# Encoder layer in split fp32: the order of copies, splits and statistics in the first feed-forward chunk

## The chip, the cores and the metric

The kernel runs on one core of one Trainium2 chip. The metric is the device time of one execution in microseconds (us), the median of three runs. Lower is better. Engines are named as in the profile: PE multiplies matrices, ACT is the scalar engine, DVE the vector engine, POOL the GpSimd engine, SP the queue that issues nearly all loads.

## The reference

One encoder layer over 256 tokens of width 2048, all in fp32. The part that the change touches is the beginning of the first line:

```python
h = h + 0.5 * swiglu(rmsnorm(h, ffn1_norm), ffn1_w_gate, ffn1_w_up, ffn1_w_down)   # D_FF = 5632
u = rmsnorm(h, mix_norm); z = u @ w_in           # neighbourhood attention, MLA, two gates
h = h + (sigmoid(gate_A) * A + sigmoid(gate_B) * Bm) @ w_out
h = h + 0.5 * swiglu(rmsnorm(h, ffn2_norm), ffn2_w_gate, ffn2_w_up, ffn2_w_down)
h = h + sigmoid(rmsnorm(h, pl_norm) @ w_pl_gate) * (p @ w_pl)
out = rmsnorm(h, final_norm)

def swiglu(x, w_gate, w_up, w_down):
    return (silu(x @ w_gate) * (x @ w_up)) @ w_down
```

## The kernel before

**Split products.** PE takes operands rounded to fp32r. Every fp32 operand is therefore split in two: `hi` is the rounded copy, made by ACT, and `lo` is what is left, subtracted by DVE (`split`, lines 87 to 89). A product is three matmuls, lo by hi, hi by hi and hi by lo (`triple`, lines 92 to 95). So each weight that comes from memory costs PE three matmuls, ACT one cast and DVE one subtraction.

**Granules.** The work is a list `grans` of granules, g0, g1 and so on, each a few tiles of weights with their matmuls. A loop over the list (the end of the function) emits for granule g its matmuls, then the small tasks that are noted for step g (`tasks[g]`, in the order in which they were noted; `at(d, fn)` notes one for d steps later), and calls `convert()`, which loads and splits weights of later granules as far as buffers W0 to W5 are free: about three granules ahead. Each engine executes its own instructions in the order in which they were emitted. The order of emission is therefore the order of every queue.

**The first chunk.** The feed-forward has 11 chunks of 512 columns. Chunk 0 is done in the plain way: g0 to g7 multiply the 16 K-tiles of the gate weights (two K-tiles a granule, 12 matmuls of 512 columns), g8 to g15 those of the up weights. The gate sums stand in PSUM banks 0 and 1, the up sums in banks 2 and 3. From g16 on, chunks 1 to 3 use a scheme with fewer products (`Block`): eight pieces of four weight tiles a chunk, five of them `Plain` (24 matmuls), three of them split over `SevenA` (9 matmuls) and `SevenB` (12). Its sums stand in banks 0 to 6. The first `Plain` granule, g16, adds first into banks 4, 5 and 6 (18 matmuls), and then into bank 3 (6 matmuls), which has to be free of the up sums by then.

**Inputs of the products.** x is transposed by PE (`plain_tiles`, four transposes into one PSUM bank), scaled by the norm's gain, and split. `first_forms(i)` does this for pair i of the eight pairs of K-tiles: tile `X{i}` gets the four plain pieces, hi and lo. The block scheme needs linear combinations too, `more_forms(i)`: DVE adds and subtracts the plain pieces into `e` (`sums`), and `e` is split into the rest of `X{i}`; the sums of pairs 2, 4 and 6 are four pieces, of the others two. The sums are taken from an fp32 copy of the plain pieces, `zs` (in buffers Z and H3), which `keep` writes from PSUM. g0 to g7 need the plain pieces of pair 0 to 7, in this order, g8 to g15 again, and g16 on need the combinations.

**Before the change.** `first_forms(i)` has ACT write hi from PSUM (line 382, two instructions), DVE write lo from PSUM (line 384, two instructions), and ACT write the fp32 copy from PSUM (line 390, two instructions). Pairs 0 and 1 are done before the loop, pairs 2 to 7 at steps 0 to 5. The statistics of the norm (`late_stat`, squares on ACT, line 413, two for each quarter of the row) stand at steps 3 to 6, the reciprocal root (`stat_done`, 14 small DVE instructions) at the end of step 6. `gate_evac` (sigmoid on ACT, one product on DVE, for each of two halves) follows the last gate matmul of g7 at once. `more_forms(0)` to `more_forms(7)` stand at steps 8 to 15, sums and split together. `gains(16, 72)`, which transposes the other norms' gains, stands at step 7. `up_evac` (line 540, two DVE instructions) follows the last up matmul of g15; two steps on, `tr(0)` and `tr(1)` transpose its result.

Of the kernel before, what the change touches and what calls it, by code (L numbers as in the profile page):

```python
# [7 lines left out]
F32 = mybir.dt.float32  # L8
F32R = mybir.dt.float32r
I32 = mybir.dt.int32  # L10
AF = mybir.ActivationFunctionType
# [3 lines left out]
P = 128  # L15
# [12 lines left out]
def encoder_kernel(ctx, tc, x, p, ffn1_norm, ffn1_w_gate, ffn1_w_up, ffn1_w_down, mix_norm, w_in,  # L28
# [8 lines left out]
    tmp = ctx.enter_context(tc.tile_pool(name="tmp", bufs=2))  # L37
    psum = ctx.enter_context(tc.tile_pool(name="psum", bufs=1, space=bass.MemoryType.PSUM))

    V, S, G, PE = nc.vector, nc.scalar, nc.gpsimd, nc.tensor  # L40
    count = [0]

    def nm(s):
        count[0] += 1
        return f"{s}_{count[0]}"
# [6 lines left out]
    def piece(tag, shape, dt=F32):  # L52
        return mem.tile(shape, dt, tag=tag, name=nm(tag))
# [10 lines left out]
    def bank():  # L64
        if seven_on[0]:
            return psum_tile(7)
        turn["side"] += 1
        return psum_tile(4 + turn["side"] % 4)
# [11 lines left out]
    tasks = {}  # L80
# [3 lines left out]
    def at(d, fn):  # L84
        tasks.setdefault(step[0] + d, []).append(fn)

    def split(hi, lo, r):
        S.copy(hi, r)  # L88
        V.tensor_tensor(out=lo, in0=r, in1=hi.bitcast(F32), op=ALU.subtract)  # L89
# [83 lines left out]
    def unit(*a, **k):  # L173
        Unit(*a, **k)
# [110 lines left out]
    for nme, g in (("ffn1", ffn1_norm), ("mix", mix_norm), ("ffn2", ffn2_norm), ("pl", pl_norm),  # L285
                   ("qa", q_a_norm), ("kva", kv_a_norm)):
        n = g.shape[-1] // P
# [7 lines left out]
    gT = cst.tile([P, 72], F32, name="gT")  # L295

    def gains(a, b):
        gps = bank()
        PE.transpose(gps[:, 0:b], grow[0:b, :], ident[0:b, 0:b])
        V.tensor_copy(gT[:, a:b], gps[:, a:b])  # L300
# [34 lines left out]
    forms = {}  # L335
# [36 lines left out]
    zs = {}  # L372

    def first_forms(i):
        p2 = plain_tiles(i)
        if i % 4 == 0:
            zs[i // 4] = piece(("Z", "H3")[i // 4], [P, 4, 4, P])
        f = piece(f"X{i}", [P, 2, 8 if i in SEVEN else 6, P], F32R)
        forms[i] = f
        hi, lo = [[f[:, b, 2 * k:2 * k + 2, :].rearrange("p a b -> p (a b)") for k in range(2)] for b in range(2)]  # L380
        for k in range(2):
            S.activation(hi[k], p2[:, k], AF.Copy, scale=gT[:, 2 * i + k:2 * i + k + 1])
        for k in range(2):
            V.scalar_tensor_tensor(out=lo[k], in0=p2[:, k], scalar=gT[:, 2 * i + k:2 * i + k + 1],
                                   in1=hi[k].bitcast(F32), op0=ALU.mult, op1=ALU.subtract)

        def keep():
            z = zs[i // 4][:, i % 4].rearrange("p (k a) b -> p k (a b)", k=2)
            for k in range(2):
                S.activation(z[:, k], p2[:, k], AF.Copy, scale=gT[:, 2 * i + k:2 * i + k + 1])  # L390
        return keep

    def more_forms(i):
        e = tmp.tile([P, 4, P], F32, tag="s", name=nm("e"))
        m = sums(zs[i // 4][:, i % 4], e, i)
        split(forms[i][:, 0, 4:4 + m], forms[i][:, 1, 4:4 + m], e[:, 0:m, :])

    def first_xop(kt):
        f = forms[kt // 2]
# [72 lines left out]
    def ffn(phase, wg, wu, wd, nxt):  # L472
        hT = {}

        def block(c):
            a = {}

            def early(q):
                a["u"], a["v"] = tmps("t")
                a["w"], a["c"] = tmps("pt")  # L480
                S.copy(a["u"], q[1])
                V.tensor_tensor(out=a["w"], in0=q[6], in1=a["u"], op=ALU.add)
                V.tensor_tensor(out=a["v"], in0=q[7], in1=a["w"], op=ALU.add)

            def late(q):
                r = rstd[phase]
                s = tmps("s")

                def first():
                    V.tensor_tensor(out=a["u"], in0=q[2], in1=a["u"], op=ALU.add)  # L490
                    V.tensor_tensor(out=a["c"], in0=q[4], in1=a["v"], op=ALU.add)

                def rest():
                    S.activation(s[0], a["u"], AF.Sigmoid, scale=r[:, 0:1])
                    S.activation(s[1], a["c"], AF.Sigmoid, scale=r[:, 1:2])
                    V.tensor_tensor(out=a["v"], in0=q[5], in1=a["v"], op=ALU.subtract)
                    V.tensor_tensor(out=a["w"], in0=q[5], in1=a["w"], op=ALU.subtract)
                    V.tensor_tensor(out=a["w"], in0=q[3], in1=a["w"], op=ALU.add)
                    for t, (g, o) in enumerate((("u", "w"), ("c", "v"))):
                        V.scalar_tensor_tensor(out=s[t], in0=a[g], scalar=r[:, t:t + 1], in1=s[t],  # L500
                                               op0=ALU.mult, op1=ALU.mult)
                        V.scalar_tensor_tensor(out=a[o], in0=a[o], scalar=r[:, t:t + 1], in1=s[t],
                                               op0=ALU.mult, op1=ALU.mult)

                    def tr(j):
                        def f():
                            if j == 0:
                                hT[c] = piece(f"H{c % 4}", [P, 2, 4, T], F32R)
                            transpose_chunk([a["w"], a["v"]], hT[c], js=(j,))
                        return f  # L510
                    at(2, tr(0))
                    at(3, tr(1))
                return first, rest
            b = Block([rows(wg, c * 512), rows(wu, c * 512)], form, early, late)

        def down_evac(n, final):
            def f(ps):
                for t in range(2):
                    hs = h[:, t, n * 512:n * 512 + 512]
                    V.scalar_tensor_tensor(out=hs, in0=ps[t], scalar=0.5, in1=hs, op0=ALU.mult, op1=ALU.add)  # L520
                if final:
                    next_norm(nxt, n)
            return f

        hold = {}

        def gate_evac(ps):
            r = rstd[phase]
            hold["a"] = tmps("t")
            for t in range(2):  # L530
                s = tmp.tile([P, 512], F32, tag="s", name=nm("s"))
                S.activation(s, ps[t], AF.Sigmoid, scale=r[:, t:t + 1])
                V.scalar_tensor_tensor(out=hold["a"][t], in0=ps[t], scalar=r[:, t:t + 1], in1=s,
                                       op0=ALU.mult, op1=ALU.mult)

        def up_evac(ps):
            r = rstd[phase]
            a = hold.pop("a")
            for t in range(2):
                V.scalar_tensor_tensor(out=a[t], in0=ps[t], scalar=r[:, t:t + 1], in1=a[t],  # L540
                                       op0=ALU.mult, op1=ALU.mult)

            def tr(j):
                def f():
                    if j == 0:
                        hT[0] = piece("H0", [P, 2, 4, T], F32R)
                    transpose_chunk(a, hT[0], js=(j,))
                return f
            at(1, tr(0))
            at(2, tr(1))  # L550

        for c0, c1 in PARTS:
            for c in range(c0, c1):
                if grans:
                    block(c)
                else:
                    unit(rows(wg, 0), 16, 512, first_xop, gate_evac)
                    unit(rows(wu, 0), 16, 512, first_xop, up_evac)
            down = len(grans)
            for n in range(4):  # L560
                def hop(kt, c0=c0):
                    d = hT[c0 + kt // 4]
                    return d[:, 0, kt % 4, :], d[:, 1, kt % 4, :]
                unit(rows(wd[c0 * 512:c1 * 512], n * 512), 4 * (c1 - c0), 512, hop,
                     down_evac(n, c1 == NC_FF), wide=True, align=(n == 0))
            m = c1 - c0
            g = grans[down:down + 2 * m]
            grans[down:down + 2 * m] = g[:m - 1] + g[m:2 * m - 1] + [g[m - 1], g[2 * m - 1]]
# [525 lines left out]
    keep = [first_forms(0)]  # L1094
    for _ in range(14):
        PE.transpose(idle[:, 0:P], ident, ident)
    for a, b in ((256, 512), (512, 1024), (1024, 1536)):
        convert()
        nc.sync.dma_start(h[:, :, a:b], xr[:, :, a:b])
        if a == 256:  # L1100
            keep.pop()()
            first_forms(1)()

    def late_stat(n):
        def f():
            stat_chunk("ffn1", n)
            if n == 3:
                stat_done("ffn1")
        return f
    for i in range(2, 8):  # L1110
        tasks.setdefault(i - 2, []).append(lambda i=i: first_forms(i)())
    for n in range(4):
        tasks.setdefault(3 + n, []).append(late_stat(n))
    for i in range(8):
        tasks.setdefault(8 + i, []).append(lambda i=i: more_forms(i))
    tasks.setdefault(7, []).append(lambda: gains(16, 72))

    for g, e in enumerate(grans):
        step[0] = g
# [58 lines left out]
```

## Time and profile before

| what | value |
|---|---|
| median of three runs | 2202.64 us (2202.17 to 2203.82) |
| profiled execution, device time | 2200.09 us |
| profiled execution, span of the trace | 2198.2 us |
| mean granted PE clock | 0.996 |
| PE busy | 2168.6 us (99%) |
| DVE busy | 1550.7 us (71%) |
| ACT busy | 1068.0 us (49%) |
| read from memory | 409.83 MB |

The span counts from the first to the last instruction that the profiler recorded. A line of the timeline has start, length, engine, line of the kernel, operation, output and inputs, count, and in square brackets the time for which the engine stood idle before it and what ended the idle time. A line of the waits has who waited, for whom, microseconds in total, times, and the longest. A line of the windows has the stretch, its length, and the busy time of PE, of its weight loads (PEld), of DVE, ACT and POOL, each with a count of instructions, then the granted PE clock, the busy share of the DMA engines and GB/s.

### The profile page before, as it was taken

How to read it: one execution, taken by the hardware profiler on the slowest of the kernel's cores; microseconds unless marked ns; L12 is line 12 of the kernel's file. 1: busy time of each engine (PE TensorE's matmuls, PEld its weight loads, DVE VectorE, ACT ScalarE, POOL GpSimd, SP SyncE). 2: the span in 40 equal slices, each digit the busy share in tenths (PEclk: the TensorE clock that was granted, in tenths of full speed). 3: DMA queues.
4: the chain of work that ended last, by engine and by line, in shares of the span. 5: the costliest groups of instructions: out<-in, count | busy, mean ns of one | idle time of the engine just before them, and what ended most of it. 6: DMA issues, size and time to landing. Idle time of an engine off the chain costs nothing. (4 is left out here: it accounts for less than half of the span.)

```text
span 2198.2 us, 24815 instructions
## 1 busy us (share of the span) xinstructions
PE 2168.6 (99%) x9789; PEld 1787.7 (81%) x9789; DVE 1550.7 (71%) x1601; ACT 1068.0 (49%) x1100; POOL 35.8 (2%) x39
## 2 busy tenths in 40 slices
PE   8899999999999999999999999999999999999997
PEld 6688888888888887788888888788888888888886
DVE  5798579975897565545655556899659994698565
ACT  6555344543555454444544445555435553455453
POOL 0000000000000000050000000000000000000000
PEclk9999999999999999999999999999999999999999
DMA  6565555565565554375455555555655666566453
GB/s 213 168 215 202 197 186 182 192 229 192 173 205 204 175 172 154 115 212 189 147 179 191 191 173 200 183 191 192 221 181 184 208 203 210 172 212 232 163 192 125
DMA packets 212003, 413.53 MB, mean 188 GB/s; under 512 B 11656, under 2 KB 12240, under 8 KB 211760
## 3 DMA queue, kind: packets, MB, share of 16 engines
q1 hardware_dynamic: 210640, 408.46, 55.8%
q0 software_dynamic: 1216, 3.50, 0.7%
q8 instruction: 76, 1.25, 0.2%
q14 instruction: 39, 0.32, 0.0%
q10 hardware_dynamic: 32, 0.01, 0.0%
HBM read 409.83 MB, written 2.10 MB: 187 GB/s over the span
## 5 line engine op out<-in xcount | busy, mean ns | idle before, releaser
L89 DVE TENSOR_TENSOR W<-R,W 128x1024 fp32r<-128x1024 f32 (+2 forms) x633 | 1008.1, 1604 | 460.6 <-ACT W L88 459.1
L88 ACT CAST W<-R 128x1024 fp32r<-128x1024 f32 (+2 forms) x633 | 855.7, 1358 | 858.7 <-DVE R L240 275.0
L93 PE MATMUL B<-W,X 128*128 128x512 f32 x2113 | 834.1, 395 | 11.3 <-DVE t L540 6.9
L95 PE MATMUL B<-W,X 128*128 128x512 f32 x2113 | 824.6, 390 | 4.4 <-DVE W L89 4.4
L94 PE MATMUL B<-W,X 128*128 128x512 f32 x2113 | 823.4, 390 | 0.0
L93 PEld LDWEIGHTS B<-W,X 128*128 128x128 f32 x2113 | 397.2, 188 | 95.9 <-DVE t L540 7.3
L95 PEld LDWEIGHTS B<-W,X 128*128 128x128 f32 x2113 | 397.0, 188 | 90.7 <-DVE W L89 7.2
L94 PEld LDWEIGHTS B<-W,X 128*128 128x128 f32 x2113 | 397.4, 188 | 80.1
L93 PE MATMUL B<-W,H 128*128 128x512 f32 x832 | 325.7, 392 | 0.0
L95 PE MATMUL B<-W,H 128*128 128x512 f32 x832 | 324.1, 389 | 0.0
L94 PE MATMUL B<-W,H 128*128 128x512 f32 x832 | 323.8, 389 | 0.0
L95 PEld LDWEIGHTS B<-W,H 128*128 128x128 f32 x832 | 156.2, 188 | 33.0 <-DVE W L89 0.4
L94 PEld LDWEIGHTS B<-W,H 128*128 128x128 f32 x832 | 156.3, 188 | 31.7
L93 PEld LDWEIGHTS B<-W,H 128*128 128x128 f32 x832 | 156.2, 188 | 31.8
L240 DVE TENSOR_TENSOR R<-R 128x1024 f32<-128x1024 f32 x63 | 77.2, 1225 | 2.2
L309 ACT CAST H<-B 128x512 fp32r<-128x512 f32 x52 | 30.1, 588 | 63.4 <-PE B L326 61.5
L310 DVE TENSOR_TENSOR H<-B,H 128x512 fp32r<-128x512 f32 x52 | 35.3, 686 | 25.1 <-ACT H L309 25.1
L520 DVE SCALAR_TENSOR_TENSOR h<-B,h 128x512 f32<-128x512 f32 x48 | 32.9, 692 | 19.5 <-PE B L95 19.5
L242 DVE TENSOR_TENSOR R<-R 128x512 f32<-128x512 f32 x63 | 43.6, 692 | 2.2
L243 DVE TENSOR_TENSOR R<-R 128x512 f32<-128x512 f32 x63 | 43.6, 692 | 2.1
L314 ACT ACTIVATE X<-B,gT 128x256 fp32r<-128x256 f32 x40 | 15.7, 476 | 35.4 <-PE B L326 35.4
L326 PE MATMUL B<-ident,t 128*128 128x128 f32 x140 | 28.4, 276 | 0.0
(221 smaller groups left out, 935.3 us busy)
## 6 DMA issues: line engine op xcount, KB each, us to landing
R<-in_ffn_w_down_dram SPq DMA_DIRECT2D x88, 1024.0 KB, 5.1
R<-in_ffn_w_gate_dram SPq DMA_DIRECT2D x170, 512.0 KB, 3.7
R<-in_ffn_w_up_dram SPq DMA_DIRECT2D x168, 512.0 KB, 4.7
R<-in_w_in_dram SPq DMA_DIRECT2D x64, 1024.0 KB, 5.2
R<-in_w_out_dram SPq DMA_DIRECT2D x16, 1024.0 KB, 5.1
R<-in_w_pl_gate_dram SPq DMA_DIRECT2D x16, 1024.0 KB, 5.1
R<-in_w_branch_a_dram SPq DMA_DIRECT2D x8, 1024.0 KB, 5.1
R<-in_w_branch_b_dram SPq DMA_DIRECT2D x8, 1024.0 KB, 5.1
```

Source lines behind the costliest of these rows:

```text
L88: S.copy(hi, r)
L89: V.tensor_tensor(out=lo, in0=r, in1=hi.bitcast(F32), op=ALU.subtract)
L93: PE.matmul(o, xl, hi, start=start, stop=False)
L94: PE.matmul(o, xh, hi, start=False, stop=False)
L95: PE.matmul(o, xh, lo, start=False, stop=stop)
L240: V.tensor_tensor(out=raw[:, 0:4:3, :], in0=raw[:, 0:3:2, :], in1=raw[:, 3:4, :].to_broadcast([P, 2, 512]), op=ALU.add)
L242: V.tensor_tensor(out=raw[:, 2, :], in0=raw[:, 0, :], in1=raw[:, 2, :], op=ALU.add)
L243: V.tensor_tensor(out=raw[:, 1, :], in0=raw[:, 2, :], in1=raw[:, 1, :], op=ALU.add)
L309: S.copy(hi, ps.rearrange("p (k t) -> p k t", k=2))
L310: V.tensor_tensor(out=lo, in0=ps.rearrange("p (k t) -> p k t", k=2), in1=hi.bitcast(F32), op=ALU.subtract)
L326: PE.transpose(ps[:, k * T + t * P:k * T + t * P + P], srcs[t][:, (2 * j + k) * P:(2 * j + k + 1) * P], ident)
L520: V.scalar_tensor_tensor(out=hs, in0=ps[t], scalar=0.5, in1=hs, op0=ALU.mult, op1=ALU.add)
```

## The change

For pairs 1 to 7 the fp32 copy is written first, and hi and lo are split from the copy, so that PSUM is read by ACT alone; pair 0 stays as it was. The squares move from steps 3 to 6 to steps 6 to 9, and the reciprocal root with them. The evacuation of the gate sums moves from step 7 to step 11. The combinations start earlier and are spread: `more_forms(0)` to `more_forms(7)` stand at steps 3, 4, 6, 7, 9, 10, 12 and 13, and the split of each comes one step after its sums. `e` takes its buffer from tag `pt` instead of `s`. `gains(16, 72)` moves from step 7 to step 14.

```diff
@@ first_forms(i)
+        z = zs[i // 4][:, i % 4]
+        z2 = z.rearrange("p (k a) b -> p k (a b)", k=2)
+
+        def keep():
+            for k in range(2):
+                S.activation(z2[:, k], p2[:, k], AF.Copy, scale=gT[:, 2 * i + k:2 * i + k + 1])
+        if i:
+            keep()
+            split(f[:, 0, 0:4], f[:, 1, 0:4], z)
+            return
         hi, lo = [[f[:, b, 2 * k:2 * k + 2, :].rearrange("p a b -> p (a b)") for k in range(2)] for b in range(2)]
         for k in range(2):
-            S.activation(hi[k], p2[:, k], AF.Copy, scale=gT[:, 2 * i + k:2 * i + k + 1])
+            S.activation(hi[k], p2[:, k], AF.Copy, scale=gT[:, k:k + 1])
         for k in range(2):
-            V.scalar_tensor_tensor(out=lo[k], in0=p2[:, k], scalar=gT[:, 2 * i + k:2 * i + k + 1],
+            V.scalar_tensor_tensor(out=lo[k], in0=p2[:, k], scalar=gT[:, k:k + 1],
                                    in1=hi[k].bitcast(F32), op0=ALU.mult, op1=ALU.subtract)
-
-        def keep():
...
         return keep

     def more_forms(i):
-        e = tmp.tile([P, 4, P], F32, tag="s", name=nm("e"))
+        e = tmp.tile([P, 4, P], F32, tag="pt", name=nm("e"))
         m = sums(zs[i // 4][:, i % 4], e, i)
-        split(forms[i][:, 0, 4:4 + m], forms[i][:, 1, 4:4 + m], e[:, 0:m, :])
+        at(1, lambda: split(forms[i][:, 0, 4:4 + m], forms[i][:, 1, 4:4 + m], e[:, 0:m, :]))
@@ ffn
         def gate_evac(ps):
+            at(4, lambda: gate_late(ps))
+
+        def gate_late(ps):
             r = rstd[phase]
@@ before the loop
             keep.pop()()
-            first_forms(1)()
+            first_forms(1)
...
     for i in range(2, 8):
-        tasks.setdefault(i - 2, []).append(lambda i=i: first_forms(i)())
+        tasks.setdefault(i - 2, []).append(lambda i=i: first_forms(i))
     for n in range(4):
-        tasks.setdefault(3 + n, []).append(late_stat(n))
+        tasks.setdefault(6 + n, []).append(late_stat(n))
     for i in range(8):
-        tasks.setdefault(8 + i, []).append(lambda i=i: more_forms(i))
-    tasks.setdefault(7, []).append(lambda: gains(16, 72))
+        tasks.setdefault(3 + (3 * i) // 2, []).append(lambda i=i: more_forms(i))
+    tasks.setdefault(14, []).append(lambda: gains(16, 72))
```

More of the change, by code (lines that the diff above doesn't have):

```diff
@@ L379, in first_forms @@
         forms[i] = f
+        z = zs[i // 4][:, i % 4]
[7 more added lines that the diff above has]
+            return
         hi, lo = [[f[:, b, 2 * k:2 * k + 2, :].rearrange("p a b -> p (a b)") for k in range(2)] for b in range(2)]
         for k in range(2):
-            S.activation(hi[k], p2[:, k], AF.Copy, scale=gT[:, 2 * i + k:2 * i + k + 1])
+            S.activation(hi[k], p2[:, k], AF.Copy, scale=gT[:, k:k + 1])
         for k in range(2):
-            V.scalar_tensor_tensor(out=lo[k], in0=p2[:, k], scalar=gT[:, 2 * i + k:2 * i + k + 1],
+            V.scalar_tensor_tensor(out=lo[k], in0=p2[:, k], scalar=gT[:, k:k + 1],
                                    in1=hi[k].bitcast(F32), op0=ALU.mult, op1=ALU.subtract)
-        def keep():
-            z = zs[i // 4][:, i % 4].rearrange("p (k a) b -> p k (a b)", k=2)
-            for k in range(2):
-                S.activation(z[:, k], p2[:, k], AF.Copy, scale=gT[:, 2 * i + k:2 * i + k + 1])
         return keep
     def more_forms(i):
-        e = tmp.tile([P, 4, P], F32, tag="s", name=nm("e"))
+        e = tmp.tile([P, 4, P], F32, tag="pt", name=nm("e"))
         m = sums(zs[i // 4][:, i % 4], e, i)
-        split(forms[i][:, 0, 4:4 + m], forms[i][:, 1, 4:4 + m], e[:, 0:m, :])
+        at(1, lambda: split(forms[i][:, 0, 4:4 + m], forms[i][:, 1, 4:4 + m], e[:, 0:m, :]))
     def first_xop(kt):
```

## The prediction

> **What bounds the kernel now.** I read the page first, then the windows of the opening 100 us, the waits in it, and last the timelines of PE, ACT and DVE.
>
> ```profile
> span 2198.2 us, 24815 instructions
> PE 2168.6 (99%) x9789; PEld 1787.7 (81%) x9789; DVE 1550.7 (71%) x1601; ACT 1068.0 (49%) x1100; POOL 35.8 (2%) x39
> ```
>
> PE is busy for 2168.6 of 2198.2 us, so all that a change of order can win is some 30 us of idle time and any time at a reduced clock. The windows show that half of it lies in the first chunk.
>
> ```profile
> 30.00:40.00 10.00, 6.12 (x26) 4.51 (x26) 3.88 (x7) 7.32 (x19) 0.00 (x0) 1.00 0.58 182
> ...
> 70.00:80.00 10.00, 5.01 (x15) 4.05 (x16) 7.83 (x12) 2.98 (x4) 0.00 (x0) 0.66 0.31 105
> 80.00:90.00 10.00, 10.00 (x48) 8.26 (x47) 7.51 (x9) 5.88 (x5) 0.00 (x0) 1.00 0.32 105
> 90.00:100.00 10.00, 10.00 (x46) 8.29 (x45) 9.32 (x8) 5.40 (x4) 0.00 (x0) 1.00 0.55 174
> ```
>
> PE was busy for 6.12 us of the stretch from 30 to 40 and for 5.01 of that from 70 to 80, where the granted clock fell to 0.66. From 80 us on it is never idle. The waits of the first 140 us name two causes:
>
> ```profile
> PE B L93 <- DVE t L540: 6.9, 1, 6.9
> ...
> ACT H L390 <- DVE X L384: 5.3, 4, 1.3
> ```
>
> The first is one stall of 6.9 us: g16 wants bank 3, and `up_evac` (line 540) has not read it. The second is the alternation in `first_forms`: ACT's copy for the sums (line 390) starts only when DVE has read the same bank (line 384). One turn of it, ACT and then DVE:
>
> ```profile
> 24.60 0.85 ACT L382 ACTIVATE X<-B,gT 128x256 fp32r<-128x256 f32 x2
> 26.79 0.84 ACT L390 ACTIVATE H<-B,gT 128x256 f32<-128x256 f32 x2 [1.34 <-DVE X L384]
> 27.51 0.63 ACT L413 ACTIVATE sq<-h 128x512 f32<-128x512 f32 x1
> ...
> 28.74 1.04 ACT L88 CAST W<-R 128x1024 fp32r<-128x1024 f32 x1
> 29.68 0.84 ACT L382 ACTIVATE X<-B,gT 128x256 fp32r<-128x256 f32 x2
> ```
>
> ```profile
> 24.74 1.23 DVE L89 TENSOR_TENSOR W<-H,W 128x1024 fp32r<-128x1024 f32 x1 [1.84 <-ACT W L88]
> 25.88 0.87 DVE L384 SCALAR_TENSOR_TENSOR X<-B,gT,X 128x256 fp32r<-128x256 f32 x2
> ```
>
> ACT writes hi at 24.60, then stands still while DVE finishes a weight split (24.74) and lo (25.88), copies at 26.79, squares at 27.51, casts the next weights at 28.74, and is at the next pair at 29.68: 5.08 us a granule. PE needs less. The next rows are windows cut at the starts of instructions, for use throughout: one granule with transposes, the work of DVE from pair 5 to the end of `up_evac`, the root of the statistics, one granule without transposes, and the stretch after the stall.
>
> ```profile
> 16.07:19.26 3.19, 3.19 (x20) 2.65 (x18) 2.01 (x3) 1.85 (x4) 0.00 (x0) 1.00 1.05 387
> 25.88:74.93 49.05, 36.90 (x157) 28.18 (x155) 31.64 (x62) 26.69 (x47) 0.00 (x0) 0.98 0.50 165
> 42.24:44.68 2.44, 2.44 (x12) 2.00 (x11) 2.06 (x16) 0.81 (x1) 0.00 (x0) 1.00 0.45 89
> 47.73:50.45 2.72, 2.72 (x14) 2.25 (x12) 1.72 (x4) 1.36 (x2) 0.00 (x0) 1.00 0.24 48
> 74.99:79.42 4.43, 4.43 (x12) 3.56 (x13) 2.97 (x4) 2.37 (x3) 0.00 (x0) 0.50 0.17 64
> ```
>
> A granule takes PE 3.19 us with the four transposes and 2.72 without (12 matmuls, 0.227 each).
>
> **The change, part by part.** Prices of DVE, from its groups between 47 and 76 us, and ACT's cast of a four-piece form:
>
> ```profile
> L89 DVE TENSOR_TENSOR W<-R,W 128x1024 fp32r<-128x1024 f32 x5 | 6.1, 1224 | 1.8 <-ACT W L88 1.8
> L89 DVE TENSOR_TENSOR W<-R,W 128x2048 fp32r<-128x2048 f32 x2 | 4.6, 2293 | 2.0 <-ACT W L88 2.0
> L89 DVE TENSOR_TENSOR X<-e,X 128x256 fp32r<-128x256 f32 x5 | 2.1, 425 | 2.4 <-ACT X L88 2.4
> L89 DVE TENSOR_TENSOR X<-e,X 128x512 fp32r<-128x512 f32 x3 | 2.1, 693 | 2.1 <-ACT X L88 2.1
> L540 DVE SCALAR_TENSOR_TENSOR t<-B,sm,t 128x512 f32<-128x512 f32 x2 | 1.4, 742 | 0.0
> L340 DVE TENSOR_TENSOR e<-Z 128x256 f32<-128x256 f32 x3 | 1.3, 418 | 0.0
> L340 DVE TENSOR_TENSOR e<-H 128x128 f32<-128x128 f32 x4 | 1.0, 282 | 0.0
> ```
>
> ```profile
> 55.41 0.62 ACT L88 CAST X<-e 128x512 fp32r<-128x512 f32 x1 [2.22 <-DVE e L347]
> ```
>
> In a row of instructions that do not wait, the next starts about 0.08 us before the last one ends on DVE (24.74 and 25.88 above) and 0.10 on ACT (28.74 and 29.68). Net steps are thus 1.14, 2.21, 0.34, 0.61, 0.66, 0.34 on DVE in the order of the rows, about 1.05 for the four dependent sums of a four-piece pair, and 0.94 for ACT's weight cast, 0.52 for its 0.62 us cast.
>
> (a) Split from the copy, pairs 1 to 7. Each pair loses two ACT writes (0.85) and two DVE subtractions from PSUM (0.87), and gains one cast (0.62) and one subtraction of 128x512 from the copy (0.69). The wait of ACT for DVE is gone. ACT then needs per granule 0.84 + 0.55 + 0.94 = 2.33 us and DVE 0.61 + 1.14 = 1.75, both under PE's 3.19. What is late next is the weights. The load for g3:
>
> ```profile
> 6.31 0.82 SPq L130 DMA_DIRECT2D H<-in_ffn_w_gate_dram  x1
> ```
>
> ```profile
> H<-in_ffn_w_gate_dram SPq DMA_DIRECT2D x1, 512.0 KB, 9.6
> ```
>
> It lands at 6.3 + 9.6 = 15.9, whatever the engines do. Cast (0.94), copies of pair 3 (0.84), their cast (0.65 with its handoff) and lo (0.75) follow one another: g3 starts at about 19.15, against 19.26 before. So the two waits saved at g1 and g2 are worth nothing. From there PE sets the pace: g6 at 19.15 + 3 x 3.19 = 28.72, and g16 at 28.72 + 10 x 2.72 + 0.23 for `gains` = 56.15. Before, by PE's rows:
>
> ```profile
> 39.98 0.50 PE L93 MATMUL B<-W,X 128*128 128x512 f32 x1 [0.33 <-ACT W L88]
> ...
> 63.72 0.39 PE L93 MATMUL B<-W,X 128*128 128x512 f32 x1
> ...
> 67.69 0.39 PE L95 MATMUL B<-W,X 128*128 128x512 f32 x1
> 74.99 0.80 PE L93 MATMUL B<-W,X 128*128 128x512 f32 x1 [6.91 <-DVE t L540]
> ```
>
> g8 began at 39.98 (here 34.2) and g16 at 63.72. PE arrives 7.6 us earlier, and after 18 more matmuls (4.1) wants bank 3 at 60.2. Whether it gets it is decided by (b) and (c).
>
> (b) Squares at steps 6 to 9. They leave the stretch where ACT turns with PE, and lengthen ACT's queue behind pair 7. Its transposes end at 29.0. From there ACT works without a gap: copies and cast of pair 7 (1.39), split of pair 1 (0.31), weights of g8 and g9 (1.88), squares (1.23), g10 (0.94), squares (1.23), split of pair 2 (0.52), g11 (0.94), squares (1.23), split of pair 3 (0.31), g12 (0.94), squares (1.33 with the read of the sum), together 12.25: the last square ends at 41.25. PE is at g9 or g10 then, and the weights of g12 and g13 are not due before 45, so PE does not notice.
>
> (c) Sums and splits a granule apart, evacuation of the gate at step 11, `gains` at 14. From the last square on it is DVE that has no gap: root of the statistics 2.44 (to 43.7), sums of pair 4 1.05, g13 1.14, sums of pair 5 0.34, lo of pair 4 0.61, g14 1.14, gate 2 x 0.66, lo of pair 5 0.34, g15 1.14, g16 2.21 (to 53.0), sums of pairs 6 and 7 1.05 and 0.34. Here ACT's cast for pair 6 (due since 54.1) holds the queue for about 0.4, lo of pair 6 takes 0.61, and the cast of g17, 1.91 us behind that of pair 6, ends at 56.6. Then g17 2.21, the copy of the gains 0.12, lo of pair 7 0.34, and `up_evac` 2 x 0.66 + 0.08: done at 60.7. Bank 3 is late by 0.5 us in place of 6.9. What stood behind the waits of ACT for sums is now a step ahead of them, so neither engine waits for the other between 41 and 54.
>
> PE goes on at 60.75 instead of 74.99: 14.2 us.
>
> (d) The clock. From 74.99 to 79.42 PE did eight matmuls and four transposes at a granted clock of 0.50. At full speed they take 8 x 0.227 + 0.47 = 2.3, so 2.1 to 2.2 us go too, if the new stall is short: the 3.9 us that PE stood idle between 30 and 40, in several waits, left the clock at 1.00. [...]
>
> (e) With one answer each, nothing: banks 0 and 1 stay taken until 49, and g18 wants them at 66; `e` from tag `pt` meets `early` at g26 only; the 0.23 of `gains` is in (a); no load moves in SP's order, each is issued when its buffer is free, thus earlier, at a DMA share of 0.50; POOL does nothing here.
>
> (f) From g16 on the program is the same, PE is never idle in it before, and its conversions wait for PE to free buffers; DVE's 9.32 of 10 fits. The gain should reach the end whole.
>
> Sum: 14.2 + 2.2 = 16.4 us. The profiled execution would have a span of 2181.8 and 2183.7 us of device time instead of 2200.09; the median of the runs stands 2.55 above that execution, so 2202.64 - 16.4 = 2186.2.
>
> **Bounds of (c).** No row shows the new order. DVE's work from pair 5's lo to the end of `up_evac` was 31.64 us in 49.05. It becomes 31.9 (three los cheaper by 0.18, sums and lo of pair 7 now inside) and starts at 24.2. Without any gap it ends at 56.1, and PE does not stall; at the share of 90 to 100 us, 0.93, at 58.5; at the old share, 0.645, at 73.7. My 60.7 is a share of 0.87, nearest to the second, because there, as in the new order, sums are not waited for by the next cast.
>
> **Rivals.**
> 1. The stall shrinks to 2.5 us or more and the clock falls again. The gain is then 16.4 - 2 - 2.2 = 12.2 or, at 4 us, 10.7: about 2191.5. For it: DVE has no slack after 41 us, and every 0.1 us there is 0.1 us of stall. Against: the queue would have to be 2 us later than its prices say. [...]
> 2. The parts of tile X are not kept apart: g12 to g15 read plain pieces of `X{4}` to `X{7}` while their combinations are still being written, and PE waits for each split. The splits of pairs 4 and 6 end near 47 and 55.4, where g12 and g14 begin at 45.0 and 50.5; some 6 us of waits replace the 0.5, gain about 11, 2191.8. Against: matmuls on the hi half of a W tile start before its lo half is written.
> 3. The alternation survives in another place, and DVE stays at its share of 0.645: `up_evac` ends at 73.7, PE goes on 1.2 us earlier at half clock, 2201.4, no difference. For: ACT and DVE keep their fixed orders. Against: the two waits it was made of are taken out.
> 4. Slower: the load for g17. `up_evac` now stands behind g17's split, whose buffer is free only when g13's split ends, at 45.9.
>
> ```profile
> R<-in_ffn_w_up_dram SPq DMA_DIRECT2D x168, 512.0 KB, 4.7
> ```
>
> It should land 0.4 + 4.7 later, at 51.0, and is wanted at 54.7. Each us beyond that is a us of stall; it is slower by 0.2% once the load lands after 54.7 + 14.2 + 4.4 = 73.3, 27 us after its issue. Nothing in the trace is that slow.
>
> **How the numbers follow.** A measurement tells about 0.2%, 4.4 us, from no change. My forecast has 0.80, with a range of its own from 2183.5 to 2190 (no stall at all and g3 a little earlier, to 2 us more stall and half of the clock's loss); rival 1 0.07, rival 2 0.05, rival 3 0.05, rival 4 0.03. Faster is the first three, 0.92, same 0.05, slower 0.03. The range from 2183 to 2192 takes in the forecast and rivals 1 and 2.
>
> **What would show it.** (a): ACT and line 390 without waits for DVE, g3 at 19.1, g6 near 28.7, g8 near 34.2. (b): last square at 41. (c): line 540 ending near 60.7 and PE's wait for it under 1 us. (d): no window under a clock of 0.9 before 100 us. (f): PE without idle time from 62 us to 200. The prediction is wrong if PE waits at g12 to g15, if line 540 ends after 64, or if waits for line 89 come up in chunks 1 to 3.

## The result, and the profile after

| | before | changed |
|---|---|---|
| median | 2202.4 us (2201.96 to 2203.82, 4 runs) | 2184.82 us (2183.91 to 2185.3, 4 runs) |
| profiled execution, device time | 2200.09 us | 2183.91 us |
| span | 2198.2 us | 2182.2 us |
| mean granted clock | 0.996 | 0.998 |

The ratio is 0.9923, with a 95% interval from 0.991 to 0.9936: 17.6 us faster by the medians, 16.0 by the spans. The forecast was 2186.2 us, 16.4 faster.

The page and the windows of the changed kernel, to be held against those of before:

```profile
span 2182.2 us, 24788 instructions
PE 2164.6 (99%) x9789; PEld 1786.8 (82%) x9789; DVE 1549.8 (71%) x1594; ACT 1066.3 (49%) x1093; POOL 35.8 (2%) x39
```

```profile
30.00:40.00 10.00, 10.00 (x46) 8.25 (x45) 8.31 (x14) 9.97 (x22) 0.00 (x0) 1.00 0.78 253
...
60.00:70.00 10.00, 9.91 (x48) 7.88 (x47) 8.41 (x10) 3.71 (x5) 0.00 (x0) 1.00 0.40 116
70.00:80.00 10.00, 10.00 (x46) 8.26 (x45) 8.78 (x8) 5.69 (x5) 0.00 (x0) 1.00 0.59 200
```

PE is busy for 10.00 us of the stretch from 30 to 40 (6.12 before). The stretch in which it resumes after bank 3, from 60 to 70, has 9.91 and a clock of 1.00, where that from 70 to 80 had 5.01 and 0.66. ACT works for 9.97 of 10 us from 30 to 40: the squares stand there now. PE's busy time in total fell by 4 us though it does the same matmuls; some 2.1 us of that are the stretch that ran at half clock (4.43 us for what takes 2.3 at full speed); where the rest comes from stays open.

The waits of the opening 140 us, and the end of DVE's queue ahead of `up_evac` (line 548 now) with PE's rows at bank 3:

```profile
ACT W L88 <- DMA H<-in_ffn_w_gate_dram: 2.9, 2, 1.6
ACT H L385 <- PE B L354: 2.2, 3, 1.0
...
PEld B L93 <- DVE t L548: 0.5, 1, 0.5
```

```profile
56.80 2.29 DVE L89 TENSOR_TENSOR W<-R,W 128x2048 fp32r<-128x2048 f32 x1 [1.12 <-ACT W L88]
59.01 0.21 DVE L300 COPY gT<-B 128x56 f32<-128x56 f32 x1
59.13 0.41 DVE L89 TENSOR_TENSOR X<-e,X 128x256 fp32r<-128x256 f32 x1
59.46 1.40 DVE L548 SCALAR_TENSOR_TENSOR t<-B,sm,t 128x512 f32<-128x512 f32 x2
```

```profile
60.44 0.39 PE L95 MATMUL B<-W,X 128*128 128x512 f32 x1
60.92 0.50 PE L93 MATMUL B<-W,X 128*128 128x512 f32 x1
```

ACT's copies (line 385 now) wait for PE's transposes and no longer for DVE: PE sets the pace. `up_evac` ends at 59.46 + 1.40 = 60.86. PE would have gone on at about 60.67, 0.227 after its last matmul, and does so at 60.92: a quarter of a microsecond is left of a wait of 6.9.

A landmark for what follows is ACT's first copy out of the block scheme's sums, far behind the first chunk and the same instruction in all kernels. The first row is of before, the second of the changed kernel:

```profile
109.23 0.58 ACT L481 COPY t<-B 128x512 f32<-128x512 f32 x1
```

```profile
93.11 0.58 ACT L486 COPY t<-B 128x512 f32<-128x512 f32 x1
```

It comes 16.12 us earlier. From it to the end of the span are 2198.2 - 109.23 = 2088.97 us before and 2182.2 - 93.11 = 2089.09 after: the gain is made in the first 93 us and arrives whole.

### The profile page after: what moved, and what is told of

It is laid out like the page before. It is cut to its first block, busy times and chain, and to the rows that moved or that the text cites. A ratio compares the mean times of both kernels' runs of the same rounds, so it can differ in the third digit from the quotient of the medians.

```text
span 2182.2 us, 24788 instructions
## 1 busy us (share of the span) xinstructions
PE 2164.6 (99%) x9789; PEld 1786.8 (82%) x9789; DVE 1549.8 (71%) x1594; ACT 1066.3 (49%) x1093; POOL 35.8 (2%) x39
## 4 chain that ended last, share of the span: by engine, by line
PE 95%; DVE 2%; ACT 1%; DMA 1%; issue 0%; SPq 0%; DVEq 0%; ACTq 0%
PE B L93 30%; PE B L95 30%; PE B L94 30%; PE B L326 1%; DVE W L89 1%; DMA H<-in_ffn_w_gate_dram 1%; PE B L753 1%; ACT W L88 1%; PE B L779 0%; PE B L778 0%; PE B L739 0%; PE B L861 0%; DMA R<-in_ffn_w_up_dram 0%; ACT sq L418 0%; ACT X L88 0%
## 5 line engine op out<-in xcount | busy, mean ns | idle before, releaser
L318 DVE SCALAR_TENSOR_TENSOR X<-B,gT,X 128x256 fp32r<-128x256 f32 x40 | 16.6, 477 | 16.5 <-ACT X L314 16.5
```

## The experiments

Ten kernels were run. The table has the median times, with the 95% interval of the ratio to the kernel before of the same runs (its medians were 2202.09 to 2202.4); the landmark; when `up_evac` ends; and PE's wait for bank 3 (from the rows and waits of each trace). In the twelve traces the first matmul of g0 starts between 7.75 and 8.72 us; where the waits ahead of it are shown, they are partly for loads (PE waits 0.5 us for x in delay_half, 0.2 in apart_only). In the seven kernels that split from the copy and load in the same order, g3 starts between 18.62 (copy_only) and 20.10 (delay_up); ahead of it ACT waits for the gate weights, 2.9 us in two waits in the changed kernel and 1.1 in one in two_only. So landmarks that differ by less than 1.5 us can't be told apart without such rows.

| kernel | time, us | ratio | landmark | `up_evac` ends | wait for bank 3 |
|---|---|---|---|---|---|
| before | 2202.4 | | 109.23 | 74.93 | 6.91 |
| changed | 2184.82 | 0.991 to 0.9936 | 93.11 | 60.86 | 0.25 |
| undo_copy | 2190.17 | 0.9931 to 0.9961 | 98.46 | 66.23 | 1.6 |
| undo_apart | 2193.96 | 0.9947 to 0.9977 | 101.65 | 66.94 | 4.12 |
| undo_late | 2186.72 | 0.9915 to 0.9949 | 94.11 | 61.62 | none |
| two_only | 2185.54 | 0.991 to 0.9939 | 92.93 | 60.53 | none |
| copy_only | 2195.95 | 0.9957 to 0.998 | 102.74 | 67.92 | 6.9 |
| apart_only | 2191.97 | 0.9934 to 0.9967 | 99.57 | 67.34 | 0.03 |
| before_banks | 2198.54 | 0.9978 to 0.9996 | 106.93 | 75.32 | not needed |
| delay_up | 2187.11 | 0.9917 to 0.9946 | 97.71 | 63.94 | 2.51 |
| delay_half | 2188.69 (one run) | | 94.52 | 62.28 | 1.32 |
| after_more | 2184.5 | 0.9907 to 0.9934 | 91.82 | 59.98 | not needed |

**undo_copy.** The changed kernel with the old `first_forms`.

```diff
-        if i:
-            keep()
-            split(f[:, 0, 0:4], f[:, 1, 0:4], z)
-            return
...
-        ...first_forms(i))
+        ...first_forms(i)())
```

> The changed kernel, with hi and lo of pairs 1 to 7 taken from PSUM again and the copy written after them. My theory (two queues in a chain: first_forms sets when PE reaches g16, and the ACT and DVE queues of sums and splits, which start from pair 7, set when bank 3 is free): the alternation of ACT and DVE comes back, 3.85 us a granule instead of 3.19 from g3 on, g8 begins near 37.9 instead of 34, up_evac ends near 66.5 instead of 60.9, PE waits some 2.4 us for bank 3, and the time is 5.6 us above the changed kernel, 2190.4. Rival (only the order of sums and splits decides when bank 3 is free, and when PE arrives does not matter): up_evac ends at 61 as in the changed kernel, 2184.8.

2190.17 us, 5.35 above the changed kernel. The alternation is back, in the waits and in the window from 30 to 40:

```profile
ACT H L385 <- DVE X L390: 5.4, 4, 1.3
```

```profile
30.00:40.00 10.00, 8.17 (x36) 5.97 (x35) 6.88 (x12) 7.40 (x16) 0.00 (x0) 1.00 0.65 211
```

`up_evac` ends 5.4 us later than in the changed kernel, as expected (66.5 forecast, 66.23 measured): the queue of sums and splits starts from pair 7, so what `first_forms` loses is passed on. PE's wait for bank 3 is 1.6 us, where 2.4 were expected. The rival, that only the order of sums and splits counts, is out.

**undo_apart.** The changed kernel, each split emitted with its sums.

```diff
-        at(1, lambda: split(forms[i][:, 0, 4:4 + m], ...))
+        split(forms[i][:, 0, 4:4 + m], ...)
```

> The changed kernel, with each split emitted together with its sums, not a step later. My theory: ACT's cast of a form stands right behind the sums it needs, the following weight cast behind that, and DVE's weight split behind both; up_evac ends near 68 instead of 60.9, PE waits 4.4 us for bank 3, 7.1 us, and since that wait is long the clock falls again, 2 us more: 2194. Rival 1 (4.4 us of idle time is not enough to lower the clock): 2192 and a granted clock of 1.00 behind the wait. Rival 2 (it is the earlier start of the sums that counts, not the gap): 2185, up_evac at 61.

2193.96 us, 9.1 above the changed kernel. PE's rows at bank 3, and the window behind them:

```profile
62.48 0.39 PE L95 MATMUL B<-W,X 128*128 128x512 f32 x1
66.99 0.79 PE L93 MATMUL B<-W,X 128*128 128x512 f32 x1 [4.12 <-DVE t L548]
67.59 0.63 PE L94 MATMUL B<-W,X 128*128 128x512 f32 x1
```

```profile
67.20:72.00 4.80, 4.80 (x14) 3.82 (x15) 4.58 (x5) 1.19 (x2) 0.00 (x0) 0.50 0.53 200
```

PE resumes 6.1 us later than in the changed kernel (66.99 against 60.92), and 4.8 us at half clock cost another 2.4. Rival 1, full clock after 4 us of idle time, is out, and so is rival 2. `e` still comes from tag `pt` here, so it is the step between sums and split that counts, not the buffer.

**undo_late.** The changed kernel with the squares at steps 3 to 6 and the gate at step 7.

```diff
-        tasks.setdefault(6 + n, []).append(late_stat(n))
+        tasks.setdefault(3 + n, []).append(late_stat(n))
...
-            at(4, lambda: gate_late(ps))
+            gate_late(ps)
```

> The changed kernel, with the squares at steps 3 to 6 and the evacuation of the gate at step 7, as before. My theory: the squares lengthen ACT's turn in g3 to g6 past PE's 3.19 us (g8 near 35.2 instead of 34.1), but the queues behind have the slack for it: up_evac ends near 62, no wait for bank 3, 1 to 1.5 us above the changed kernel, 2186, which the times can hardly tell and the traces can. Rival (taking the statistics and the gate out of the way is what unblocks the two queues): up_evac after 65, 2189 or more.

2186.72 us, 1.9 above the changed kernel by the medians; the intervals of the two ratios overlap. `up_evac` ends at 61.62, 0.8 later than in the changed kernel, and PE does not wait for bank 3. In the trace PE is idle for 0.95 us between 30 and 50, where the changed kernel has none, and the landmark is 1.0 later. This edit is worth about 1 us at most, within what a trace varies by.

**two_only.** The kernel before with the split from the copy and the split of a form a step later (`e` from tag `pt`), and nothing else.

> The kernel before with two edits alone: hi and lo of pairs 1 to 7 split from the copy, and the split of a form one step after its sums (e from tag pt). Sums at steps 8 to 15, squares at 3 to 6, gate at 7 and gains at 7 stay as before. My theory: these two carry the whole gain; g8 near 35.1, up_evac near 61, no wait for bank 3, within 1 us of the changed kernel, 2185. Rival (the earlier and spread sums are needed too, since four of the sums are still to be done after g11): a wait of 3 us or more for bank 3, 2189 or more.

2185.54 us, with nearly the changed kernel's interval. Its landmark is 92.93 against 93.11, and PE is idle for 0.28 us between 30 and 90:

```profile
30.00:40.00 10.00, 9.72 (x43) 7.68 (x42) 7.98 (x21) 8.13 (x17) 0.00 (x0) 1.00 0.83 280
60.00:70.00 10.00, 10.00 (x50) 8.27 (x49) 9.54 (x12) 5.12 (x7) 0.00 (x0) 1.00 0.23 85
```

Two of the edits carry the whole gain that the times can tell. The later statistics, the later gate, the spread sums and the moved `gains` are not needed for it.

**copy_only** and **apart_only.** The kernel before with one of the two.

> The kernel before with one edit: hi and lo of pairs 1 to 7 split from the copy. My theory: g8 begins near 35 instead of 40, but sums and splits still alternate from step 8 on, up_evac ends near 69, PE reaches bank 3 earlier and still waits 7 us there, at half clock behind it: the gain is 6.7 us, 2195.6. Rival (the whole shift of PE is worth its 8 us at g16 and the wait at bank 3 shrinks too, since the queues start earlier): 2190 or less. Rival 2 (the wait for bank 3 grows by all that PE gains): 2202.

> The kernel before with one edit: the split of a form comes one step after its sums (e from tag pt), sums at steps 8 to 15 as before. My theory: the start of the chunk stays as it was (g8 near 40), up_evac ends near 67.8 instead of 74.9, the wait for bank 3 shrinks from 6.9 to about 1 us, and the clock stays at 1.00: 8.2 + 2.2 = 10.4 us, 2192. Rival (without the earlier start of the queues the gap only moves the wait elsewhere): less than 4 us, 2198 or more.

2195.95 and 2191.97 us: 6.3 and 10.3 below the kernel before of the same runs (2202.22), where 6.7 and 10.4 were expected. With the copy alone PE comes earlier, `up_evac` ends 7 us earlier, and PE waits as long as before:

```profile
PE B L93 <- DVE t L548: 6.9, 1, 6.9
```

With the gap alone the start stays as it was (PE busy for 6.33 of the 10 us from 30 to 40), and the wait is gone, where about 1 us was expected:

```profile
30.00:40.00 10.00, 6.33 (x29) 4.73 (x28) 4.03 (x6) 7.33 (x19) 0.00 (x0) 1.00 0.52 164
...
70.00:80.00 10.00, 10.00 (x47) 8.25 (x46) 8.61 (x9) 6.29 (x7) 0.00 (x0) 1.00 0.29 97
```

```profile
67.14 0.39 PE L95 MATMUL B<-W,X 128*128 128x512 f32 x1
67.40 0.50 PE L93 MATMUL B<-W,X 128*128 128x512 f32 x1
```

The two sum to 16.5 us, about what both do together. They act on two stretches one after the other, the copy on that before pair 7 and the gap on that behind it. The copy also shortens the work of a pair, on ACT from 0.85 to 0.62 us and on DVE from 0.87 to 0.69; how much of the 6.3 us comes from that, and how much from the end of the alternation, was not separated.

**before_banks.** Is the wait of 6.9 us a matter of bank 3? The kernel before, with gate sums in banks 2 and 3, up sums in 0 and 1, and the transposes of the result put off (they stood one and two steps behind `up_evac`).

```diff
-    turn = {"acc": 0, "side": 0, "raw": 0}
+    turn = {"acc": 2, "side": 0, "raw": 0}
...
-            at(1, tr(0))
-            at(2, tr(1))
+            at(4, tr(0))
+            at(5, tr(1))
```

> The kernel before with the PSUM banks of the first chunk exchanged (gate sums in banks 2 and 3, up sums in 0 and 1) and tr(0) and tr(1) put off by three steps, so that g16 no longer needs the bank that up_evac reads. Rival theory (the stall of 6.9 us is a matter of bank 3): the stall and the slow clock go, 9 us, 2193. My theory (the stall is the backlog of DVE and ACT, which bank 3 only makes visible): up_evac still ends near 75, the weights of g17 to g20 come late instead, in waits of 1 to 2 us each; only the clock is saved, since no wait is long: 2 to 3 us, 2199.8, granted clock 1.00 throughout.

2198.54 us, 3.7 below the kernel before, not 9. `up_evac` ends at 75.3 as before. PE runs on past bank 3 and meets late weights:

```profile
71.75 0.50 PE L95 MATMUL B<-W,X 128*128 128x512 f32 x1 [1.45 <-DVE W L89]
77.53 0.50 PE L93 MATMUL B<-W,X 128*128 128x512 f32 x1 [0.46 <-ACT W L88]
79.32 0.54 PE L95 MATMUL B<-W,X 128*128 128x512 f32 x1 [1.06 <-DVE W L89]
79.65 0.63 PE L93 MATMUL B<-W,X 128*128 128x512 f32 x1
80.08 0.63 PE L94 MATMUL B<-W,X 128*128 128x512 f32 x1
```

PE's waits between 60 and 90 us come to 3.6 us, and the matmuls at 0.63 us cost some 1.7, 5.3 together, in place of 6.9 and 2.1. So the backlog of ACT and DVE was the cause, and bank 3 the place where it showed. One part of the expectation failed: the clock did not stay at 1.00. From 79.6 on, behind waits none of which is above 1.5 us, matmuls take 0.63 us, and the granted clock is 0.53 from 79.6 to 83.2. The experiment does not price the clock by itself, therefore.

**delay_up** and **delay_half.** The changed kernel with four or two additions on DVE ahead of `up_evac`; their results are not used.

```diff
+            d = tmps("s")
+            for k in range(4):      # 2 in delay_half
+                V.tensor_tensor(out=d[k % 2], in0=h[:, k % 2, 0:512], in1=h[:, k % 2, 512:1024], op=ALU.add)
```

> The changed kernel with four needless additions of 128x512 on DVE right ahead of up_evac, 0.61 to 0.69 us each, 2.5 us in all. My theory (up_evac is at the end of a queue without slack): PE's wait for bank 3 grows from 0.3 to 2.8 us, and the time by 2.5 us, 2187.3; whether the clock falls too shows where its threshold lies, 0.3 to 2.8 us of idle time being possibly still too little, in which case it stays at 1.00 (if it falls, 2189.5). Rival (DVE has slack there): no change, 2184.8.

> The changed kernel with two needless additions of 128x512 on DVE ahead of up_evac instead of four, 1.2 us. If a wait of 2.5 us is near the edge at which the clock falls, a wait of about 1.5 us leaves it at 1.00, and the first evacuation of the block scheme comes 1.2 us later than in the changed kernel, at 94.3 (plus what the launch is late). If any wait there lowers the clock, it falls here too, and it comes 2 to 3 us later still.

PE's rows, of delay_up and then of delay_half:

```profile
63.99 0.50 PE L93 MATMUL B<-W,X 128*128 128x512 f32 x1 [2.51 <-DVE t L551]
64.33 0.50 PE L94 MATMUL B<-W,X 128*128 128x512 f32 x1
64.63 0.63 PE L95 MATMUL B<-W,X 128*128 128x512 f32 x1
```

```profile
62.34 0.50 PE L93 MATMUL B<-W,X 128*128 128x512 f32 x1 [1.32 <-DVE t L551]
62.67 0.40 PE L94 MATMUL B<-W,X 128*128 128x512 f32 x1
```

The wait grows by what DVE is given, to 2.51 and 1.32 us: no slack stands ahead of `up_evac`. After 2.51 us the clock falls (0.63 us a matmul from the third one on, a granted clock of 0.73 from 64 to 65 us and 0.71 from 65 to 70), after 1.32 it does not (0.39 to 0.40 us a matmul from the second one on, a granted clock of 1.00 from 60 to 65). The landmark of delay_half, 94.52, is 1.4 later than in the changed kernel, of which 1.1 are the wait and 0.2 a later start of g3 (19.67), as expected; that of delay_up, 97.71, is 4.6 later, of which 2.3 are the wait, 0.6 a later start (g3 at 20.10 against 19.47), and some 1.7 the clock. The time of delay_up is only 2.3 above that of the changed kernel, and its four runs spread from 2185.49 to 2190.03; whether the clock fell in each of them their mean granted clocks, 0.996 to 0.999, do not tell. delay_half has one time alone, 2188.69, too few to hold against it; its span, 2185.6, is 1.2 below that of delay_up's profiled execution.

**after_more.** The experiments point to little that is left: the quarter of a microsecond at bank 3, and the wait for the weights of g3. The banks are exchanged as above, `tr` is one step later, and the last quarter of x is loaded behind the weights of g3.

```diff
-        if g == 0:
+        if g == 1:
             nc.sync.dma_start(h[:, :, 1536:2048], xr[:, :, 1536:2048])
```

> The changed kernel with two edits more: the banks of gate and up sums exchanged and tr(0), tr(1) one step later, which takes the wait at bank 3 away; and the last quarter of x loaded behind the weights of g3 instead of ahead of them. My theory: g3 starts about 0.8 us earlier, since its weights land about 1.3 us earlier (512 KB at the 385 GB/s of that stretch), up_evac ends near 60, g16 runs without a wait: 1 to 2 us in the trace at the first evacuation of the block scheme (93.1 in the changed kernel, 91.1 to 92.1 here), 2183.3, too little for the times to tell. Rival (the load of x that moves is what first_forms then waits for, or the exchanged banks make chunk 1 wait): 2186 or more.

In the trace ACT casts the weights of g3 at 14.07 without a wait for their load, and g3 starts at 18.60 instead of 19.47, though g0 started 0.4 later; `up_evac` ends at 59.98, PE has no wait there, and the landmark is at 91.82, 1.3 earlier. How much of this is the edit's is not shown: copy_only, with the old order of loads, has g3 at 18.62. The time, 2184.5 us, can't be told from the changed kernel's. It beats the kernel before by 17.6 us (ratio 0.9907 to 0.9934) and is no shown gain over the changed one.

## Why the prediction was right

**(a) Split from the copy.** The step that mattered was what comes next once the alternation is gone. ACT and then PE at g3 in the changed kernel:

```profile
16.25 1.05 ACT L88 CAST W<-H 128x1024 fp32r<-128x1024 f32 x1 [1.62 <-DMA H<-in_ffn_w_gate_dram]
17.20 0.84 ACT L385 ACTIVATE Z<-B,gT 128x256 f32<-128x256 f32 x2
18.07 0.62 ACT L88 CAST X<-Z 128x512 fp32r<-128x512 f32 x1
```

```profile
19.47 0.50 PE L93 MATMUL B<-W,X 128*128 128x512 f32 x1 [0.60 <-DVE X L89]
```

The weights of g3 land at 16.25 (15.9 forecast), and g3 starts at 19.47 (19.15 forecast, 19.26 before): all that was won in g1 and g2 is lost there, and PE sets the pace from then on: g6 at 29.09, g8 at 34.66, g16 at 56.59, some 0.4 behind the forecast each (28.72, 34.2, 56.15). That the load holds g3 fits after_more, where it lands earlier and PE is not idle ahead of g3. That 15.9 came so near was partly luck: in the seven kernels with the split from the copy and this order of loads g3 starts between 18.62 (copy_only) and 20.10 (delay_up). Less the 3.22 us from 16.25 to 19.47 in the changed kernel, its weights land between 15.40 and 16.88, an estimate.

**(b) The squares.** The last one ends at 41.66, 41.25 forecast. The chain of prices on ACT was right. Its purpose was not tested by the prediction: undo_late and two_only show that the squares could have stayed.

**(c) The gap.** `up_evac` was forecast to end at 60.7 and ended at 60.86. The last square came 0.4 late and the end 0.16, so small errors cancelled on the way. PE wanted bank 3 at 60.67 and not at 60.2, which is why the wait is 0.25 and not 0.5. DVE was busy for 31.26 of the 36.37 us from pair 5's lo to there, a share of 0.86 (0.87 forecast, 31.9 us of work). The other shares that bounded it, 1 and 0.645, were far off; carrying both queues row by row came nearer. delay_up and delay_half show that this end is what PE waits for.

**(d) The clock.** With a wait of 0.25 us it stayed at 1.00 (60 to 70 us), and undo_apart shows the loss come back with a wait of 4.12 us (0.50 from 67.2 to 72). Rival 1 was nearer than thought: it asked for a wait of 2.5 us or more, and delay_up fell after 2.51.

**(f) The rest.** 2089.09 us behind the landmark, 2088.97 before. PE is busy for 138.00 of the 138 us from 62 to 200. Nothing is given back, though DVE is busy for 90% of that stretch.

Rival 2 (parts of tile X not kept apart) did not come: PE has no wait in g12 to g15. Rival 3 did not come: DVE's share is 0.86, not 0.645. The load of rival 4, for g17, was not late: ACT casts it at 54.86 right behind the cast for pair 6.

The sum, 16.4 us, is 16.0 to 16.2 in the profiled executions. The medians differ by 17.6, but by the interval of the ratio anything from 14.1 to 19.8 fits. In the twelve traces the stretch behind the landmark varies from 2088.6 us (undo_copy) to 2091.8. The two kernels with exchanged banks are at the upper end (2091.7 and 2091.8), the others reach 2091.1; whether the exchange costs anything there, and what makes the rest of the difference, stays open.

What the prediction did not do is divide the gain among the edits. It treated (b), the later gate and the spread sums as parts of one mechanism. copy_only, apart_only and two_only show two mechanisms, 6.3 and 10.3 us, and nothing measurable in the others.

## What to carry to other kernels

When an engine waits for a buffer, first ask whether the reader of that buffer is late by itself or at the end of a queue: here exchanging the buffer (before_banks) brought 3.7 us, putting the queue in order (apart_only) 10.3. Where two engines that work off their queues in the order of emission hand work to each other, emit the second half of each handoff a step later, so that neither stands at its head waiting for the other; the two lines of apart_only did most of this change (ACT's waits for `e` in the first 140 us fell from 8.8 + 8.5 to 7.0 + 0.8 us). And carry the queues forward with the durations of the trace: a queue of some 32 us on two engines (from the last transposes at 29.0 to the end of `up_evac`) came out within 0.2 us, with errors of some 0.4 us on the way.

## What the hardware showed beyond that

The granted clock fell behind idle time of different lengths. Behind single waits it was 0.50 after 6.91 us (before, 74.99 to 79.42) and after 4.12 (undo_apart, 67.2 to 72), and after 2.51 (delay_up) it had a mean of 0.71 from 65 to 70; in copy_only, with 6.9, it was 0.67 from 60 to 70 us and 0.82 from 70 to 80. In before_banks it was 0.53 from 79.6 to 83.2, behind waits of 1.45, 0.46 and 1.06 us, 3.0 in 9 us. Yet single waits of 1.32 us (delay_half) and 1.6 (undo_copy) left the clock at 1.00 (from 60 to 65 and from 60 to 70), and the kernel before kept 1.00 between 30 and 40 with 3.9 of 10 us idle:

```profile
31.49 0.50 PE L93 MATMUL B<-W,X 128*128 128x512 f32 x1 [1.61 <-DVE X L384]
36.56 0.50 PE L93 MATMUL B<-W,X 128*128 128x512 f32 x1 [2.06 <-DVE X L384]
```

No threshold on the longest wait or on the idle share of 10 us fits all of these; what the fall goes by was not settled here. In these five traces with a fall PE then worked at about half clock for 3.3 us (delay_up, from 64.63 to 67.97, where a matmul takes 0.39 us again) to some 5.6 us (copy_only, an estimate: from about 68.0, right behind `up_evac`, to 70, and 3.6 us of the ten from 70 to 80, whose mean is 0.82). By before, 4.43 us for what takes 2.3, that cost some 1.6 to 2.7 us, an estimate too.
